# Moving the first weight chunk ahead of the activations, and a tile's transposes behind two chunks

## The chip, the cores and the metric

One core of one Trainium2 chip. The metric is the device time of one execution in microseconds; the time of a kernel is the median of several executions. Engines are TensorE (PE in the profile, its weight loads PEld), VectorE (DVE), ScalarE (ACT), GpSimd (POOL) and SyncE (SP), which issues most DMAs.

## The reference

A matrix product and a rotary embedding of each head. Shapes: x is 16 x 512 x 768, weight 768 x 768, cos and sin 512 x 64, all float32, with 12 heads of 64.

```python
y = np.matmul(x, weight).reshape(batch, seq, n_heads, head_dim)
y1, y2 = y[..., :32], y[..., 32:]
out1 = y1 * cos1 - y2 * sin1
out2 = y2 * cos2 + y1 * sin2
out = np.concatenate([out1, out2], axis=-1).reshape(batch, seq, hidden)
```

cos1, cos2, sin1, sin2 are the two halves of cos and sin, one row for each sequence position.

## The kernel before

x is worked on in 64 tiles of 128 rows by 768 columns, four tiles to a group of 16. A tile goes through these steps: it is loaded as float32 (`load`, 384 KB), cast to float16 (`castx`, on ScalarE), transposed by TensorE into PSUM in six blocks of 128 x 128 and copied from there to SBUF (`turn`, whose second argument names the engine of the copy), and multiplied by the weight. The weight is cut into six chunks of 128 rows (w0 to w5, 384 KB each, `load_w`), each cast to float16 by `cast_w`. The product of a tile is the sum over the six chunks. The tile's products lie in PSUM banks of 512 columns; `rope` multiplies them by cos and sin on VectorE and adds the two halves on GpSimd, and `store` issues the result's DMA.

Every engine works through its own instructions in the order in which the program gives them. The helper `Flow.do` gives each instruction the semaphore waits that follow from what it reads and writes, so an instruction that waits holds up what stands behind it on its engine. All loads of the first stage stand in SyncE's queue in the order of the list `order` (L441), then cos and sin, then further tiles of x, as `pump` sends them.

The first group (tiles 0 to 3) is written out by hand (L509 to L534), because the weight arrives chunk by chunk at the same time. `mm0(i, c)` multiplies tile i by chunk c in two matmuls, one of 512 columns and one of 256. `warm(k)` issues k matmuls on a tile of zeros. The order there, engine by engine:

- TensorE: nine warm matmuls, transposes of tile 0, three warm matmuls, transposes of tile 1, tiles 0 and 1 by w0, transposes of tile 2, tiles 0 and 1 by w1, then by w2, tile 2 by w0 and w1, transposes of tile 3, tile 2 by w2, then tiles 0, 1 and 2 by w3 and by w4. Behind the list come tiles 0, 1 and 2 by w5 (L591 to L593) and tile 3, with the transposes of tiles 4 and 5 between.
- VectorE: the copies of tiles 0 and 1, then the casts of w0 to w5, then two instructions that build the table from cos and sin (L535 to L539), then the products of `rope`.
- ScalarE: the casts of tiles 0, 1 and 2, the copy of tile 2, the cast of tile 3, the copy of tile 3, then casts and copies of later tiles in turn.

From tile 4 on (the loop after L602) TensorE multiplies with half-height matmuls (`both`, `steps`, profile line L349), transposes come from `turn_rows` (L257) and, for some pairs of tiles, from VectorE. Profile lines of the helpers: L176 is every cast and copy (`copy`), L196 the load of a tile of x, L218 that of a weight chunk, L242 the transposes of `turn`, L324 the matmuls of `mm0`, L394 the products and L410 the additions of `rope`.

## Time and profile before

| what | value |
|---|---|
| median of 3 executions | 154.4 us (154.16 to 154.4) |
| the profiled execution, in all | 154.73 us |
| its span, first to last instruction | 152.9 us |
| granted TensorE clock, mean | 0.994 |
| bytes moved | 51.27 MB, mean 335 GB/s |
| first x tile cast (ScalarE) begins | 4.24 us |
| w0 cast (VectorE) begins | 7.67 us |
| w5 cast begins | 14.49 us |
| first product of rope (VectorE) begins | 15.83 us |

The span and all positions are of the one profiled execution; the median is of other executions of the same kernel. In the views, L and a number is a line of the kernel, a name such as "xt<-pt" says what is written from what, and the time in brackets is how long the engine was idle before the instruction and what ended that. A wait for several things is put down to the one that came last.

### The profile page before, as it was taken

Reading aid. Unit: us, or ns where it says so; the run is one execution under the profiler, and the core shown is the slowest. Engines: PE = TensorE matmul, PEld = TensorE weight load, DVE = VectorE, ACT = ScalarE, POOL = GpSimd, SP = SyncE. Lnnn points to the kernel's source line nnn. Section 1 sums busy time; section 2 is a strip of 40 time slices with the busy share of each in tenths; the row PEclk is TensorE's granted clock in tenths of the full one; section 3 lists DMA queues with packets and bytes.
Section 4 is the critical chain, followed back from the end, with each engine's and each line's share of the span. In section 5 each row is a group of like instructions: output and inputs, shape, how many; then the busy total and the mean of one; then the engine's idle time right before and its main releaser. Section 6 shows DMA issues by size and latency. Waiting matters only on the chain.

```text
span 152.9 us, 4416 instructions
## 1 busy us (share of the span) xinstructions
PE 141.5 (93%) x1944; PEld 102.7 (67%) x1944; DVE 129.3 (85%) x119; ACT 78.7 (51%) x92; POOL 124.6 (81%) x81
## 2 busy tenths in 40 slices
PE   6669997999999999999999999999999999999930
PEld 2325674777777778777777777777777777766720
DVE  0244995888888999999999999999999999978980
ACT  3444778879778843556263726273526735461000
POOL 1000299599999999999999999999997979799970
PEclk9999999999999999999999999999999999999997
DMA  3999999999999999999999999999999998550992
GB/s 124 350 395 404 400 402 385 385 380 257 363 358 352 368 336 353 349 400 340 339 341 392 364 336 339 372 370 334 345 360 407 416 403 323 233 210 0 374 354 97
DMA packets 27555, 51.27 MB, mean 335 GB/s; under 512 B 7184, under 2 KB 13072, under 8 KB 27536
## 3 DMA queue, kind: packets, MB, share of 16 engines
q1 hardware_dynamic: 13504, 24.78, 46.8%
q10 hardware_dynamic: 8592, 24.25, 40.3%
q0 software_dynamic: 5440, 1.97, 10.4%
q8 instruction: 15, 0.25, 0.6%
q14 instruction: 4, 0.03, 0.1%
HBM read 27.79 MB, written 25.17 MB: 346 GB/s over the span
## 4 chain that ended last, share of the span: by engine, by line
PE 86%; DMA 5%; DVE 3%; SPq 1%; ACT 1%; issue 1%; DVEq 0%
PE py L349 72%; PE py L324 8%; DMA w_raw<-in_weight_dram 5%; PE pt L257 4%; PE pt L242 1%; DVE w_raw L394 1%; SPq L196 1%; DVE ov L410 1%; SPq L218 1%; ACT xc L176 1%; ACT xt L176 1%; DVE xs L394 0%; DVE w_sb L176 0%; DVE tq L394 0%; DVEq L57 0%
## 5 line engine op out<-in xcount | busy, mean ns | idle before, releaser
L349 PE MATMUL py<-w_sb,xt 64*128 64x512 f16 (+1 forms) x864 | 95.6, 323 | 0.0
L410 POOL TENSOR_TENSOR ov<-tq 128x1024 f32<-128x1024 f32 (+2 forms) x33 | 68.9, 2109 | 19.3 <-DVE tq L394 19.1
L394 DVE TENSOR_TENSOR tq<-py,csn 128x1024 f32<-128x1024 f32 (+2 forms) x56 | 68.1, 1253 | 3.6 <-PE py L349 3.1
L349 PEld LDWEIGHTS py<-w_sb,xt 64*128 64x128 f16 x864 | 58.8, 94 | 17.2
L349 PE MATMUL py<-w_sb,xp 64*128 64x512 f16 (+1 forms) x480 | 61.9, 323 | 0.0
L176 ACT COPY xt<-pt 128x768 f16<-128x768 f16 x42 | 33.5, 799 | 39.4 <-PE pt L257 27.3
L176 ACT CAST xc<-xs 128x768 f16<-128x768 f32 x44 | 39.1, 902 | 21.1 <-DMA xs<-in_x_dram 17.2
L394 DVE TENSOR_TENSOR w_raw<-py,csn 128x1024 f32<-128x1024 f32 (+1 forms) x38 | 45.3, 1191 | 5.3 <-PE py L349 3.7
L410 POOL TENSOR_TENSOR ov<-w_raw 128x1024 f32<-128x1024 f32 (+2 forms) x22 | 44.3, 2027 | 3.4 <-DVE w_raw L394 3.2
L349 PEld LDWEIGHTS py<-w_sb,xp 64*128 64x128 f16 x480 | 35.5, 94 | 9.9
L324 PE MATMUL py<-w_sb,xt 128*128 128x256 f16 (+1 forms) x96 | 15.5, 313 | 1.9 <-DVE w_sb L176 1.7
L257 PEld LDWEIGHTS pt<-ident,xc 64*128 64x128 f16 x432 | 13.7, 95 | 2.7 <-ACT xc L176 1.4
L324 PEld LDWEIGHTS py<-w_sb,xt 128*128 128x128 f16 x96 | 8.7, 98 | 7.5 <-DVE w_sb L176 3.2
L257 PE MATMUL pt<-ident,xc 64*128 64x64 f16 x432 | 12.6, 190 | 1.1 <-ACT xc L176 1.1
L211 POOL DMA_DIRECT2D xh<-in_x_dram x20 | 11.7, 594 | 0.0
L176 ACT CAST xd<-xb 128x1536 f16<-128x1536 f32 x5 | 8.2, 1630 | 1.5 <-DMA xb<-in_x_dram 1.4
L176 DVE CAST w_sb<-w_raw 128x768 f16<-128x768 f32 x6 | 3.4, 560 | 4.4 <-DMA w_raw<-in_weight_dram 4.4
L285 DVE STREAM_TRANSPOSE xp<-xh 128x768 f32<-128x768 f32 x5 | 6.2, 1235 | 0.0
L492 PE MATMUL py<-cold 128*128 128x512 f16 x12 | 4.3, 518 | 1.4 <-DVE cold L435 1.4
L176 DVE COPY xt<-pt 128x768 f16<-128x768 f16 x2 | 1.1, 557 | 4.9 <-PE pt L242 4.9
L285 DVE STREAM_TRANSPOSE xp<-xd 128x768 f32<-128x768 f32 x5 | 4.8, 969 | 0.0
L242 PEld LDWEIGHTS pt<-ident,xc 128*128 128x128 f16 x48 | 3.0, 98 | 2.7 <-ACT xc L176 1.8
(16 smaller groups left out, 13.2 us busy)
## 6 DMA issues: line engine op xcount, KB each, us to landing
out_dram<-ov ACTq DMA_DIRECT2D x30, 768.0 KB, 8.8
xs<-in_x_dram SPq DMA_DIRECT2D x44, 384.0 KB, 15.9
xb<-in_x_dram SPq DMA_DIRECT2D x20, 192.0 KB, 18.0
w_raw<-in_weight_dram SPq DMA_DIRECT2D x6, 384.0 KB, 7.8
xh<-in_x_dram POOLq DMA_DIRECT2D x20, 96.0 KB, 13.7
out_dram<-ov SPq DMA_DIRECT2D x1, 384.0 KB, 3.1
out_dram<-ov ACTq DMA_DIRECT2D x1, 384.0 KB, 2.8
out_dram<-ov SPq DMA_DIRECT2D x1, 256.0 KB, 2.1
```

The costliest lines, as they stand in the source:

```text
L176: eng.copy(out=o, in_=i_) if e == "act" else eng.tensor_copy(out=o, in_=i_)
L196: do(e, lambda eng: eng.dma_start(out=xs_b[k], in_=x[b].rearrange("(p r) h -> r p h", r=SB)[r]), writes=[f"xs{k}"], dma=f"xs{k}")
L211: do(e, lambda eng: eng.dma_start(out=dst[ts(q, R)], in_=src[r, q]), writes=[f"{name}q{q}"], dma=name)
L218: do(e, lambda eng: eng.dma_start(out=w_raw[:, t, h], in_=wv[t, h]), writes=[f"wr{t}{h}"], dma=f"w{t}{h}")
L242: do("pe", lambda eng: eng.transpose(pt[:, t, h, :], src[:, t, h, :], ident), reads=[f"xc{c}", "ident"], writes=[f"pt{k}"], tick=(t, h) == ...
L257: do("pe", lambda eng: eng.transpose(pts[r][:, t, h, :], src[rows, t, h, :], ident[rows, rows]), reads=[f"xc{c}", "ident"], writes=[f"pt{r ...
L285: do("dve", lambda eng: eng.transpose(out=dst, in_=src), reads=rd, writes=[f"xp{z}"])
L324: do("pe", lambda eng: eng.matmul(ps, get(t, h), w_sb[:, t, h, a - s * H : z - s * H], start=start, stop=stop), reads=[key, f"w{t}{h}"], w ...
L349: do("pe", lambda eng: eng.matmul(py[:, lo:hi], get(t, h)[rows], w_sb[rows, t, h, lo - s * H : hi - s * H], start=opens, stop=r == 1 and s ...
L394: do("dve", lambda eng: eng.tensor_tensor(out=tq.rearrange("p j (h d) -> p j h d", d=D), in0=ps.rearrange("p (h d) -> p h d", d=D) .unsque ...
L410: do(adder, lambda eng: eng.tensor_tensor(out=ov_b[o][:, ds(c0, w)].rearrange("p (h t d) -> p h t d", t=2, d=HD), in0=tq[:, 0].rearrange(" ...
L492: do("pe", lambda eng: eng.matmul(py[:, ts(b, 512)], cold[:, 0:P], cold, start=True, stop=warmed[0] < WARM - 6), reads=["cold"], writes=[f ...
```

## The change

w0 is issued ahead of all tiles of x. Its cast moves on VectorE to the front, ahead of the copies of tiles 0 and 1. On TensorE tiles 0 and 1 are multiplied by w0 and w1 before the transposes of tile 2. The copy of tile 2 moves from ScalarE to VectorE, where it stands between the casts of w1 and w2. Tile 2 is multiplied by w0 and w1 before tiles 0 and 1 are multiplied by w2. What follows the transposes of tile 3 stays.

```diff
-    order = [0, 1, "w0", 2, "w1", "w2", 3, "w3", "w4", "w5"]
+    order = ["w0", 0, 1, "w1", 2, "w2", 3, "w3", "w4", "w5"]
...
     U0 = units(0)
     warm(9)
+    cast_w(CHUNKS[0], "dve")
     castx(0, "act")
     turn(0, "dve")
     castx(1, "act")
     warm(3)
     turn(1, "dve")
     castx(2, "act")
-    cast_w(CHUNKS[0], "dve")
     for i in (0, 1):
         mm0(i, CHUNKS[0])
-    turn(2, "act")
+    cast_w(CHUNKS[1], "dve")
+    for i in (0, 1):
+        mm0(i, CHUNKS[1])
+    turn(2, "dve")
     castx(3, "act")
-    for c in CHUNKS[1:3]:
-        cast_w(c, "dve")
-        for i in (0, 1):
-            mm0(i, c)
+    cast_w(CHUNKS[2], "dve")
     for c in CHUNKS[:2]:
         mm0(2, c)
+    for i in (0, 1):
+        mm0(i, CHUNKS[2])
     turn(3, "act")
     mm0(2, CHUNKS[2])
     for c in CHUNKS[3:5]:
```

## The prediction

> **What bounds the kernel now.** I read the page first: span, busy shares, chain by line.

> ```profile
> span 152.9 us, 4416 instructions
> PE 141.5 (93%) x1944; PEld 102.7 (67%) x1944; DVE 129.3 (85%) x119; ACT 78.7 (51%) x92; POOL 124.6 (81%) x81
> ...
> PE 86%; DMA 5%; DVE 3%; SPq 1%; ACT 1%; issue 1%; DVEq 0%
> ```

> TensorE is busy 93% of the span and holds 86% of the chain that ends last; all the DMA on that chain is the load of one weight chunk. So the steady part is TensorE's, and the edit, which lies before 16 us, is worth what it does to the moment at which TensorE's unbroken run reaches a given instruction. The chain in order of time shows where that run begins and the only place where it breaks again before the tail:

> ```profile
> 3.28 7.27 DMA w_raw<-in_weight_dram
> ...
> 10.57 0.57 DVE w_sb L176
> ...
> 11.19 1.47 PE py L324 x8
> 12.66 0.33 PE pt L242 x6
> 12.99 4.24 PE py L324 x26
> ...
> 23.42 0.80 ACT xt L176
> 24.22 0.80 ACT xc L176
> ```

> Columns are start, length, what. The DMA step ends at 10.54: this is chunk w2. From 11.19 TensorE goes on without a wait: eight matmuls, the transposes of tile 3, 26 matmuls. A unit for later: one tile times one chunk is two matmuls, so 26 matmuls are 13 units in 4.24 us, 0.326 us each; one tile's transposes take 0.33.

> Next the timeline of the first 18 us, VectorE, ScalarE and weight loads, for landings and slack (start, length, instruction; in brackets the idle time before it and what ended it):

> ```profile
> 4.24 1.84 ACT L176 CAST xc<-xs 128x768 f16<-128x768 f32 x2 [2.05 <-DMA xs<-in_x_dram]
> 6.77 0.56 DVE L176 COPY xt<-pt 128x768 f16<-128x768 f16 x1 [0.43 <-PE pt L242]
> 7.67 0.56 DVE L176 CAST w_sb<-w_raw 128x768 f16<-128x768 f32 x1 [0.34 <-DMA w_raw<-in_weight_dram]
> 8.62 0.87 ACT L176 CAST xc<-xs 128x768 f16<-128x768 f32 x1 [2.55 <-DMA xs<-in_x_dram]
> 9.58 0.56 DVE L176 CAST w_sb<-w_raw 128x768 f16<-128x768 f32 x1 [1.35 <-DMA w_raw<-in_weight_dram]
> 10.10 0.80 ACT L176 COPY xt<-pt 128x768 f16<-128x768 f16 x1 [0.60 <-PE pt L242]
> 14.49 0.56 DVE L176 CAST w_sb<-w_raw 128x768 f16<-128x768 f32 x1 [0.45 <-DMA w_raw<-in_weight_dram]
> 15.11 1.74 PEld L324 LDWEIGHTS py<-w_sb,xt 128*128 128x128 f16 x12 [0.23 <-DVE w_sb L176]
> 17.16 0.34 PEld L242 LDWEIGHTS pt<-ident,xc 128*128 128x128 f16 x6 [0.31 <-ACT xc L176]
> ```

> A cast starts some 0.02 us after its transfer lands, so by place in the queue the landings are about 4.22 (place 1), 5.17 (place 2: issued at 1.39, 3.8 us to landing), 7.65 (3, now w0), 8.60 (4, x2), 9.56 (5, w1), 10.54 (6, w2), then about 0.97 apart to 14.47 (10, w5). One interval is out of line: place 3 comes 2.48 us after place 2 instead of 0.95, so 1.53 us late, and all later places keep that lag. Two more things are to be seen. The load of w5's first weights begins at 15.11, just when w5's cast (14.49 + 0.56, and 0.06 that TensorE takes to start) is done: TensorE, from 11.19, needs 0.65 + 0.65 + 0.33 + 0.33 + 0.98 + 0.98 = 3.92 us to come to w5, that is 15.11. There is **no slack**, and a faster head alone gains nothing while w5 lands at 14.47. And tile 4's transposes at 17.16 wait for ScalarE's cast of x4 (16.22 to 17.11): six units after 15.11 would be 17.07, so a head that is late gets 0.09 us back there.

> In whole-microsecond windows the traffic of the lag is seen (busy of each engine, then granted clock, DMA share, GB/s):

> ```profile
> 4.00:5.00 1.00, 0.93 (x4) 0.19 (x2) 0.00 (x0) 0.76 (x1) 0.00 (x0) 1.00 0.99 387
> 5.00:6.00 1.00, 0.74 (x8) 0.56 (x9) 0.21 (x1) 0.93 (x2) 0.00 (x0) 1.00 1.03 338
> 6.00:7.00 1.00, 0.73 (x8) 0.42 (x6) 0.57 (x2) 0.08 (x1) 0.00 (x0) 1.00 0.96 289
> 9.00:10.00 1.00, 0.56 (x7) 0.34 (x6) 0.42 (x1) 0.49 (x1) 0.00 (x0) 1.00 1.02 406
> ```

> **The change, part by part.** *The queue order.* All ten transfers are 384 KB and go through SyncE's queue; w0 goes from place 3 to 1, x0 to 2, x1 to 3, w1 from 5 to 4, x2 from 4 to 5; w2 to w5, x3 and all behind keep place and bytes. I take the landings by place, because the dip to 338 and 289 GB/s lies at a time (5 to 7 us) when transfers of both kinds are under way, and because x and w transfers keep the same 0.95 to 0.98 us spacing afterwards. Bounds for x1, which takes place 3: 6.12 if the lag belonged to w0 standing there (5.17 + 0.95), 8.60 if it slipped a further place. I use 7.65, the row of that place.

> *The early cast of w0* (0.56 us) runs at 4.24 to 4.80, while VectorE would idle until the first transposes are done: nothing. Behind it in VectorE's order stands the copy of tile 0, not due before 6.65; w0 would have to land after 6.0 to cost anything.

> *The path through x1.* x0: cast 5.19 to 6.07, transposes 6.12, copy done 7.21, beside the wait for x1. x1: cast 7.67 to 8.54 (0.87), transposes from 8.60, copy 0.54 after their start (as 9.55 to 10.10 now), 9.14 to 9.70. w1's cast, landed at 8.60, stands behind that copy in VectorE's order: 9.72 to 10.28. TensorE does tile 1 by w0 at 9.76, both tiles by w1 from 10.34 to 10.99, and only then, in its own order, tile 2's transposes; x2's cast (9.58 to 10.45) has been ready for half a microsecond. VectorE's copy of tile 2 starts at 11.53 and ends at 12.09 (ScalarE needs 0.80 for it now, so VectorE saves 0.24, which is in the sum). TensorE goes on at 12.15 with tile 2 by w0 and w1.

> *The path through w2.* Its cast, ready at 10.54, now stands in VectorE's order behind the copy of tile 2, which waits for transposes: 12.11 to 12.67 instead of 10.57 to 11.13. Waiting for it is TensorE alone, at 12.80, after tile 2 by w0 and w1; so this wait costs nothing, with 0.07 us of cover. Without cover it would cost its 0.56.

> From 12.15 the same 3.92 us of work stand between TensorE and w5 as now from 11.19: the same units in another order. So w5 begins at 16.07 instead of 15.11: **+0.96**, and at tile 4's transposes 0.09 of it is regained: **+0.87**. The moved copy takes 0.80 us from ScalarE, which idles there (0.65 to 2.55 us before each of its casts there): nothing. VectorE's first product, now at 15.83 and tied to cos and sin, would come at 16.7, so 0.9 late with TensorE; TensorE's next use of those banks, now at 18.94, comes after VectorE's release at 18.12, and both shift together. The break at 23.4 doesn't swallow it: the two ScalarE steps there (copy, cast) begin when TensorE's own transposes end. After 25.07 the chain is TensorE to the tail.

> [...] The copy of a transposed tile out of PSUM took 0.56 us on VectorE and 0.80 on ScalarE in the rows above. [...]

> The sum against the profiled execution: 152.9 span, 154.73 in all, would become 153.8 and 155.6. The median of the runs shown is 154.4, 0.33 below that execution; on it the forecast is 154.4 + 0.87 = **155.3 us**.

> **Rivals.** (a) *x1 in time, x2 late.* If x1 lands by 6.8, the path through x2 decides: place 5 is 0.96 later than place 4. x2 9.56, cast to 10.45, transposes 10.50, copy to 11.60, TensorE 11.66 instead of 11.19: +0.47 - 0.09 = +0.38, 154.8. For it: the lag's lost bytes (62 and 111 of some 400 GB/s over 1 us each) are only 0.43 us of all the queues together, so it may sit elsewhere next time. Against it: place 3 had the lag.

> (b) *The lag goes away: faster.* If the lag belongs to the first weight rows being read behind two tiles of x, then w0 at place 1 takes it into the start-up, and places 3 to 10 land up to 1.53 us sooner: x1 at 6.12, and the whole computed path with it. Then +0.87 - 1.53 = -0.66, 153.7; it decides from x1 before 6.78 and x2 before 9.18. For it: the transfer with the lag is the first one of the weight. Against it: the dip goes on at 6 to 7 us, when x2 and w1 are due, and a queue with the same bytes is no shorter.
> [...]

> (c) *Later still.* w0's first read costs at the start and the lag comes too: x1 between 7.95 and 8.60, the sum between +1.2 and +1.8, 155.6 to 156.2. For it: only that place 1 has not been a weight before.

> (d) *Nothing*, if a later stage gives it all back: 154.4. Only the 23.4 us break could, and it follows TensorE.

> **How the numbers follow.** Forecast (+0.6 to +1.15, 155.0 to 155.55) 48%; (a) 18%; (b) 23%; (c) 8%; (d) 3%. The time is the forecast's. What can be told from no change is 0.2%, 0.31 us. Slower: 48 + 12 of (a) + 8 = 68%. Same: 6 of (a), 3 of (b), 3 of (d) = 12%. Faster: 20 of (b). The range runs from (b)'s full price, 153.7, to 155.6, where (c) begins; about 10% is left out, most of it (c).

> **What would show it.** Right: x1's cast near 7.67 and not 6.1; copies of tiles 1 and 2 near 9.1 and 11.5; w2's cast beginning right behind the latter though w2 lands at 10.5; w5's first weights near 16.0 with no wait on their cast; tile 4's transposes near 18.0 without a wait; the same gap near 24; tail unchanged, span 153.8. Wrong: x1's cast before 6.8, which brings (a) or (b), told apart by w5's landing (14.5 or near 13); a wait of TensorE for w2 would make it 0.1 or more worse.

## The result, and the profile after

| | before | changed |
|---|---|---|
| median of 20 executions | 154.39 us (153.21 to 156.32) | 155.0 us (154.37 to 155.81) |
| ratio, 95% interval | | 1.0052 (1.0031 to 1.0072) |
| the profiled execution, in all | 154.73 us | 154.79 us |
| its span | 152.9 us | 153.0 us |

The ratio is 0.80 us (0.48 to 1.11) on 154.4: slower, by half a per cent. It is taken over fast executions alone (none over 1.5% above a kernel's fastest); the medians, of all 20, are 0.61 us apart. But the profiled execution of the changed kernel is only 0.06 us longer than that of before, and the 20 times fall into two groups of ten, 154.37 to 154.79 and 155.22 to 155.81. The profile is of the lower group. Both facts have to be explained.

The page of the changed kernel, span and chain by engine:

```profile
span 153.0 us, 4416 instructions
...
PE 83%; DVE 4%; DMA 3%; POOL 3%; ACT 2%; issue 1%; SPq 1%; ACTq 0%; DVEq 0%
```

VectorE, GpSimd and ScalarE have entered the chain at TensorE's cost. Where, the chain in order of time shows (start, length, what):

```profile
1.86 4.96 DMA xs<-in_x_dram
6.85 0.89 ACT xc L176
...
10.71 0.57 DVE xt L176
...
11.32 1.48 PE py L324 x8
...
15.95 2.30 DVE tq L394
...
18.33 4.70 POOL ov L410 x2
...
23.05 0.42 ACTq L431
...
23.51 0.80 ACT xt L176
24.30 0.80 ACT xc L176
...
25.15 0.35 PE pt L257 x12
```

Instead of w2's load, the load of x1 starts the chain. TensorE's run with tile 2 begins at 11.32 behind VectorE's copy of that tile (10.71), where w2's cast at 10.57 released it before. The timeline has the landings (start, length, instruction, idle time before and what ended it):

```profile
6.85 0.88 ACT L176 CAST xc<-xs 128x768 f16<-128x768 f32 x1 [0.82 <-DMA xs<-in_x_dram]
9.23 0.88 ACT L176 CAST xc<-xs 128x768 f16<-128x768 f32 x1 [1.50 <-DMA xs<-in_x_dram]
8.80 0.55 DVE L176 CAST w_sb<-w_raw 128x768 f16<-128x768 f32 x1
11.18 0.55 DVE L176 CAST w_sb<-w_raw 128x768 f16<-128x768 f32 x1
14.13 0.56 DVE L176 CAST w_sb<-w_raw 128x768 f16<-128x768 f32 x1 [0.43 <-DMA w_raw<-in_weight_dram]
```

x1 landed at 6.83, not at 7.65; x2 at 9.21; w5's cast began at 14.13 instead of 14.49. So this execution's loads had a smaller lag than those of the profile before, by 0.36 us. That hides the cost. TensorE's rows of the loop over tiles 4 and up (its first matmul of L349) and of the transposes behind the break, in the profile before:

```profile
18.94 1.89 PE L349 MATMUL py<-w_sb,xt 64*128 64x512 f16 x10
25.07 0.35 PE L257 MATMUL pt<-ident,xc 64*128 64x64 f16 x12 [1.07 <-ACT xc L176]
```

and in the changed one:

```profile
18.94 1.90 PE L349 MATMUL py<-w_sb,xt 64*128 64x512 f16 x10
25.15 0.35 PE L257 MATMUL pt<-ident,xc 64*128 64x64 f16 x12 [1.15 <-ACT xc L176]
```

The loop begins at 18.94 in both. Counted from the start of w5's cast, which carries the whole lag, it begins after 4.45 us before and after 4.81 now, and the transposes behind the break come after 10.58 and 11.02. **Freed of the lag, the change costs 0.36 us at the loop and 0.44 behind the break.** This distance is the measure used below.

### The profile page after: what moved, and what is told of

Its sections match the earlier page's. It is cut to its first block, busy times and chain, and to the rows that moved or that the text cites. A ratio compares the mean times of both kernels' runs of the same rounds, so it can differ in the third digit from the quotient of the medians.

```text
span 153.0 us, 4416 instructions
## 1 busy us (share of the span) xinstructions
PE 141.8 (93%) x1944; PEld 102.9 (67%) x1944; DVE 129.5 (85%) x120; ACT 78.1 (51%) x91; POOL 124.6 (81%) x81
## 4 chain that ended last, share of the span: by engine, by line
PE 83%; DVE 4%; DMA 3%; POOL 3%; ACT 2%; issue 1%; SPq 1%; ACTq 0%; DVEq 0%
PE py L349 70%; PE py L324 7%; PE pt L257 4%; DMA xs<-in_x_dram 3%; POOL ov L410 3%; DVE tq L394 2%; PE pt L242 1%; ACT xc L176 1%; DVE w_raw L394 1%; DVE xt L176 1%; DVE ov L410 1%; ACT xt L176 1%; DVE xs L394 0%; SPq L196 0%; ACTq L431 0%
## 5 line engine op out<-in xcount | busy, mean ns | idle before, releaser
L349 PE MATMUL py<-w_sb,xt 64*128 64x512 f16 (+1 forms) x864 | 95.6, 323 | 0.0
L349 PEld LDWEIGHTS py<-w_sb,xt 64*128 64x128 f16 x864 | 58.8, 94 | 17.3
L349 PE MATMUL py<-w_sb,xp 64*128 64x512 f16 (+1 forms) x480 | 61.9, 323 | 0.0
L176 ACT COPY xt<-pt 128x768 f16<-128x768 f16 x41 | 32.8, 800 | 44.1 <-PE pt L257 31.2
L176 ACT CAST xc<-xs 128x768 f16<-128x768 f32 x44 | 39.2, 903 | 18.6 <-DMA xs<-in_x_dram 14.4
L349 PEld LDWEIGHTS py<-w_sb,xp 64*128 64x128 f16 x480 | 35.5, 94 | 9.9
L324 PE MATMUL py<-w_sb,xt 128*128 128x256 f16 (+1 forms) x96 | 15.6, 313 | 1.0 <-DVE xt L176 1.0
L324 PEld LDWEIGHTS py<-w_sb,xt 128*128 128x128 f16 x96 | 8.9, 98 | 6.4 <-DVE xt L176 1.5
L176 ACT CAST xd<-xb 128x1536 f16<-128x1536 f32 x5 | 8.2, 1634 | 0.0
L176 DVE CAST w_sb<-w_raw 128x768 f16<-128x768 f32 x6 | 3.3, 556 | 4.1 <-DMA w_raw<-in_weight_dram 4.1
L242 PEld LDWEIGHTS pt<-ident,xc 128*128 128x128 f16 x48 | 3.0, 98 | 3.5 <-issue 1.6
L176 DVE COPY xt<-pt 128x768 f16<-128x768 f16 x3 | 1.7, 557 | 4.4 <-PE pt L242 4.4
L242 PE MATMUL pt<-ident,xc 128*128 128x128 f16 x48 | 4.0, 220 | 1.4 <-ACT xc L176 1.4
```

The source lines that it names most:

```text
L176: eng.copy(out=o, in_=i_) if e == "act" else eng.tensor_copy(out=o, in_=i_)
L242: do("pe", lambda eng: eng.transpose(pt[:, t, h, :], src[:, t, h, :], ident), reads=[f"xc{c}", "ident"], writes=[f"pt{k}"], tick=(t, h) == ...
L324: do("pe", lambda eng: eng.matmul(ps, get(t, h), w_sb[:, t, h, a - s * H : z - s * H], start=start, stop=stop), reads=[key, f"w{t}{h}"], w ...
L349: do("pe", lambda eng: eng.matmul(py[:, lo:hi], get(t, h)[rows], w_sb[rows, t, h, lo - s * H : hi - s * H], start=opens, stop=r == 1 and s ...
```

## The experiments

Of each profiled execution (us; "distance" is from the start of w5's cast to the loop's first matmul):

| kernel | x1 landed | w5's cast | loop | distance | in all |
|---|---|---|---|---|---|
| before | 5.17 | 14.49 | 18.94 | 4.45 | 154.73 |
| before, again | 5.26 | 14.43 | 18.84 | 4.41 | 155.19 |
| changed | 6.83 | 14.13 | 18.94 | 4.81 | 154.79 |
| changed, again | 6.71 | 13.91 | 18.72 | 4.81 | 154.75 |
| changed, third | 6.42 | 13.79 | 19.62 | 5.83 | 155.42 |
| loads' order alone | 6.46 | 13.67 | 18.39 | 4.72 | 154.88 |
| order of work alone | 5.67 | 13.85 | 18.98 | 5.13 | 155.61 |
| copy on ScalarE | 6.58 | 13.75 | 18.93 | 5.18 | 155.18 |
| x1 later | 8.04 | 14.51 | 20.86 | 6.35 | 156.91 |
| more warm matmuls | 7.03 | 13.88 | 19.04 | 5.16 | 154.88 |

### Each part alone

The order of the loads alone: the kernel before with

```diff
-    order = [0, 1, "w0", 2, "w1", "w2", 3, "w3", "w4", "w5"]
+    order = ["w0", 0, 1, "w1", 2, "w2", 3, "w3", "w4", "w5"]
```

> Only the order of the loads is changed (w0 ahead of all tiles of x, x2 at place 5); the order of work on the engines is that of before. My theory (the time is set by when TensorE has tile 2, and a queue place is worth 0.96 us): TensorE, which transposes tile 2 ahead of tiles 0 and 1 by w1, waits for x2's cast; with landings as in the profile of before, transposes at 10.50, w1's matmuls 10.83 to 11.48, w2's at 11.48 instead of 11.19, so +0.29 and 0.09 regained at tile 4: +0.2 us against before. Rival (the moved loads are the whole cost, the reordered work costs nothing): +0.6 us, as the full change.

Distance 4.72, so +0.27 against 4.45, near the +0.2 of the theory, but by another wait (TensorE's rows):

```profile
9.14 0.82 PE L324 MATMUL py<-w_sb,xt 128*128 128x512 f16 x4 [1.12 <-DVE w_sb L176]
9.80 0.50 PE L242 MATMUL pt<-ident,xc 128*128 128x128 f16 x6
```

Tile 2's transposes didn't wait for x2's cast, which was done at 9.68. TensorE had waited for w0's cast: w0 landed at 4.57, but in the old order of work its cast stands on VectorE behind the copies of tiles 0 and 1, and began at 8.54. Both paths came to tile 2 within 0.1 us of each other, so the agreement is luck. The time, 154.52 against 154.88 (ratio 0.9981, 0.9927 to 1.0036), can't tell +0.2 from nothing, but speaks against +0.6.

The order of work alone: the changed kernel with the old line `order`.

> Only the order of work on the engines is changed; the loads stand as before. My theory: tile 2's transposes wait behind tiles 0 and 1 by w1, whose cast ends at 10.14, so they begin at 10.85 instead of 9.55, the copy ends at 11.95 and the unbroken run of TensorE, from tile 2 by w0 on, begins at 12.0 instead of 11.19: +0.8 less 0.09, +0.7 us against before. Rival (the loads are the whole cost): 0.0. A second rival, that the copy on VectorE is what costs: then w2's cast, behind it in VectorE's order, would be waited for by TensorE; I expect no such wait.

Distance 5.13, +0.68, as expected; the time doesn't contradict (1.0032, 0.9964 to 1.0101). There was no wait for w2's cast. So each half costs by itself, 0.27 and 0.68 (one execution of each), and the two together only 0.36. In the new order of work tile 2's transposes wait for tiles 0 and 1 by w1, and the new loads bring w1 a place sooner; with the new loads w0 is early, and the new order of work casts it early. Each half needs the other.

### The same kernels again

> The kernel before, unaltered, for a second profile. My theory: from the start of w5's cast to the first matmul of the loop 4.45 us again, 0.36 below the changed kernel, whatever the lag of the loads is in this execution; the lag itself (w5's cast at 14.49 in the first profile, 13.67 to 14.14 in the others) moves by some tenths from execution to execution. Rival: the figure moves with the lag.

4.41 with a lag nearly like the first's: it agrees, though it hardly tests the rival. What tests it is the whole table: with the first group of before (also in the three kernels further down that leave it as it is) the distance is 4.40 to 4.45 while w5's cast moves from 13.86 to 14.49. TensorE stood still in this execution behind a late load near 117 us (in the chain the load ends at 116.09 and TensorE goes on at 117.78), which is why it took 155.19.

> The changed kernel, unaltered, for a second profile: where do x1, w1 and x2 land in another execution? My theory of the two groups of its times (near 154.7 and near 155.5): they differ in x1's landing; an execution near 154.7 has x1 before 6.9 and tile 2 set by x2, one near 155.5 has x1 near 7.65 and TensorE coming to tile 2 by w0 near 12.1. Rival: the groups differ in the tail or the steady part, and the first 18 us are alike.

Again the lower group (154.75): distance 4.81, x1 at 6.71. No execution of the upper group was caught yet.

### The copy's engine, and x1's place

```diff
-    turn(2, "dve")
+    turn(2, "act")
```

> The changed kernel with the copy of tile 2 back on ScalarE. My theory (tile 2's path from x2's landing, then TensorE's unbroken run): the copy takes 0.80 instead of 0.56, so TensorE's run begins 0.24 later against the loads; from the start of w5's cast to the first matmul of the loop 4.81 + 0.24 = 5.05 us. Rival (w2's cast, which stands behind the copy on VectorE, is what TensorE waits for): with the copy gone from VectorE the cast comes sooner and the figure falls below 4.8.

5.18: later by 0.37, where 0.24 was expected from the copy. Here TensorE came to tile 2's transposes at 9.93, and x2's cast had ended at 9.74. x0 had landed only at 5.64, and its transposes (6.67) and the three warm matmuls behind them held up those of tile 1 to 7.65. So the path through the first tiles set the time, and this is the other 0.13. The sign settles it: w2's cast was free sooner and nothing got faster, so that wait costs nothing, and VectorE is the cheaper place for this copy (0.56 us there, 0.80 on ScalarE).

x1 a place further back:

```diff
-    order = ["w0", 0, 1, "w1", 2, "w2", 3, "w3", "w4", "w5"]
+    order = ["w0", 0, "w1", 1, 2, "w2", 3, "w3", "w4", "w5"]
```

> The changed kernel with x1 one place further back: w0, x0, w1, x1, x2, the rest as it is. It makes the case that the prediction forecast, tile 1 late. My theory: TensorE's unbroken run begins 4.50 us after x1 lands; x1 lands 5.84 us ahead of w5, so from the start of w5's cast to the first matmul of the loop it is 4.81 + 1.45 = 6.3 us, less at most 0.1. Rival: only the order of work on the engines counts, 4.8.

6.35, but not for the reason given. Here w5's cast was itself held up in VectorE's order, to 14.51 though w5 landed at 13.86; from the landing the loop is 7.0 us away. By x1's landing TensorE should have come to tile 2 by w0 at 12.4 to 12.5 and came at 13.25. The missing 0.8 us is in the windows of this run (busy of each engine, then granted clock, DMA share, GB/s):

```profile
8.00:9.00 1.00, 0.01 (x1) 0.01 (x1) 0.00 (x0) 0.87 (x1) 0.00 (x0) 0.71 0.98 387
9.00:10.00 1.00, 1.00 (x7) 0.75 (x8) 0.15 (x1) 0.88 (x1) 0.00 (x0) 0.50 1.05 421
10.00:11.00 1.00, 0.99 (x4) 0.21 (x3) 0.87 (x2) 0.08 (x1) 0.00 (x0) 0.50 1.01 406
11.00:12.00 1.00, 1.00 (x5) 0.58 (x5) 0.00 (x0) 0.80 (x1) 0.00 (x0) 0.59 1.05 421
12.00:13.00 1.00, 0.60 (x8) 0.32 (x5) 0.36 (x1) 0.00 (x0) 0.00 (x0) 1.00 1.01 384
```

The clock granted to TensorE fell to 0.50 between about 8.4 and 11.8 us (0.71 over one microsecond is 0.58 us at half clock, 0.59 is 0.82 us), while tile 1 was late and TensorE had stood idle for 1.5 us (busy for 0.51 between 7 and 8 us, 0.01 between 8 and 9). A theory that the prediction didn't have: **the gaps that the change opens in TensorE's first microseconds act on its clock.**

### The upper group

> The changed kernel, unaltered, for a third profile. From the start of w5's cast to the first matmul of the loop 4.81 us again; x1 lands before 7.1 again and tile 2's copy is released by the path through x2. If this execution is of the group near 155.5, it has a wait of 0.5 to 0.8 us behind a load near 117 us that the two profiles near 154.8 don't have; the rival is a later head.

This execution, 155.42 (one more beside the 20), is of the upper group, and the rival is right: no wait behind a load near 117 us, but a distance of 5.83. x1 was early (6.42), so the theory that the groups differ in its landing falls. TensorE's rows of this run:

```profile
6.34 0.80 PE L242 MATMUL pt<-ident,xc 128*128 128x128 f16 x6 [0.92 <-ACT xc L176]
6.93 1.49 PE L492 MATMUL py<-cold 128*128 128x512 f16 x3
8.21 0.85 PE L242 MATMUL pt<-ident,xc 128*128 128x128 f16 x6
...
10.86 0.50 PE L242 MATMUL pt<-ident,xc 128*128 128x128 f16 x6
```

and the first three of the same in the first profile of the changed kernel:

```profile
6.17 0.49 PE L242 MATMUL pt<-ident,xc 128*128 128x128 f16 x6 [0.88 <-ACT xc L176]
6.50 0.81 PE L492 MATMUL py<-cold 128*128 128x512 f16 x3
7.78 0.51 PE L242 MATMUL pt<-ident,xc 128*128 128x128 f16 x6 [0.47 <-ACT xc L176]
```

The same instructions take 0.80, 1.49 and 0.85 instead of 0.49, 0.81 and 0.51. From start to start the three warm matmuls are 0.43 us apart here and 0.22 there: TensorE still runs at half the rate it has there. In this execution tile 1's transposes wait not for x1's cast, done at 7.32, but for TensorE's slow work ahead of them; tile 2 by w0 begins at 12.01 instead of 11.1 to 11.3, and the loop 0.68 to 0.90 us later than in the other two.

The column of the granted clock in the views shows 1.00 from the start in all these runs (in the third also from 7 to 8 us, where the warm matmuls are 0.43 us apart) but hides the half rate: the trace's record of the clock begins with its first rise. That rise stands at 4.29 and 4.16 us in the two profiles of before, and at 5.02, 5.92 and 10.08 in the three of the changed kernel. Between the nine warm matmuls and tile 0's transposes TensorE was idle for 0.75 to 0.92 us in these three, because x0 lands a place later (its cast begins at 5.16 to 5.33 instead of 4.24 and 4.36); in the two of before, that gap was 0.33 and 0.52 us.

The changes of the clock in these records have a spacing. With x1 later the clock is up from 5.00 to 8.41, at half from there to 11.82 and up again: 3.41 us each. In the 13 other profiles the time from its rise to its fall behind the last matmuls is 41 to 44 times 3.413 us (146.77 us, in the first profile of either kernel, is 43 times). What sets this spacing, no run shows. But each profile can be laid out in stretches of 3.413 us, back from the rise, and the share of each that matmuls fill can be read from the trace:

| execution | stretch (us) | filled by matmuls | the clock at its end |
|---|---|---|---|
| before | 0.87 to 4.29 | 0.84 | rises |
| changed | 1.60 to 5.02 | 1.00 | rises |
| changed, again | 2.50 to 5.92 | 0.86 | rises |
| changed, third | 3.25 to 6.66 | 0.73 | stays down |
| changed, third | 6.66 to 10.08 | 1.00 | rises |
| x1 later | 5.00 to 8.41 | 0.42 | falls |

In all 14 profiles the stretch that ends at a rise is filled to 0.81 or more, and none filled to 0.73 or less ends at one. Once up, the clock stayed up behind stretches of 0.46 and more. In the third execution a stretch took in the whole gap, and the clock rose one stretch later. My reading of these profiles: **where the stretches fall against the gap makes the two groups.**

The 20 executions bear this out. In the profiles the clock falls to half behind the last matmuls at the end of such a stretch and stays there, so the span and the mean clock of an execution give an estimate of the time of the fall: 153.0 - 2 x 0.004 x 153.0 = 151.8 us for the profiled one, where the trace has 151.79. Carried back by whole stretches (good to about 0.15 us), each execution has one stretch that ends between 4.08 and 7.49 us. In eight it ends behind 6.05 us, with most or all of the gap inside, and all eight are of the upper group (155.44 to 155.81). Of the other twelve, ten are of the lower group. The two that are not took 155.73, with an end at 4.15 (TensorE starts at 1.41, so that stretch is filled to 0.80, between the 0.73 and the 0.81 of the profiles), and 155.22, with 5.71, which stays open. The kernel before shows no such split: of its 55 executions that are compared in the experiments, 28 have the end behind 6.05 and a median of 154.40, the other 27 one of 154.56.

A half clock alone isn't enough: with the old first group it was seen twice (tile 0's transposes 0.80 us, in the kernel with tiles 7 and 8 cast sooner and in the one with the pairs on SyncE, further down) and cost nothing, distances 4.44 and 4.42, because the clock had risen by tile 1's transposes (0.50) and the work behind waits for loads there (TensorE was idle for 1.12 us ahead of tiles 0 and 1 by w0 in the former). To test it, the gap was filled:

```diff
-    WARM = 12
+    WARM = 14
...
-    warm(9)
+    warm(11)
```

> The changed kernel with eleven warm matmuls ahead of tile 0's transposes instead of nine. In the third profile of the changed kernel the transposes of tile 0 took 0.80 us and the three warm matmuls 1.49, against 0.49 and 0.81 in the other two: TensorE still ran at half clock there, after it had stood idle from 5.4 to 6.3 us, and came 0.7 us later to the loop. My theory: the group near 155.5 is made of such executions, and the idle time that w0's place in front opens is what keeps the clock down in them; two more matmuls of 0.43 us at half clock fill it to about 6.1 us, so the clock is up by 7 us in every execution, the distance from w5's cast to the loop is 4.8 to 4.9 and times between 155.2 and 155.9 come only with late loads: the median is 0.3 to 0.5 us below the changed kernel's 155.0 against the same kernel before, that is a ratio to before of 1.002 to 1.004 instead of 1.0052. Rival: the clock's rise has nothing to do with the idle time; the ratio stays at 1.005 or, as the added matmuls hold up tile 0, grows.

Ratio to before 1.0011 (0.9981 to 1.0040), below the 1.002 to 1.004 expected, median 154.68 against 154.45. Of the 11 executions that are compared, ten lie between 154.42 and 155.14 and one at 155.68, so the upper group is nearly gone; its profile has the rise at 5.88 and the full clock at tile 0's transposes (0.49). Three of the 11 have their stretch end at 6.48, 6.78 and 7.00, where the changed kernel had upper executions alone, and they took 154.65, 155.00 and 154.62; the one at 155.68 isn't among them (5.28). (One further execution took 307.86 us; it wasn't profiled and its cause is open.) Its distance of 5.16 is more than the 4.8 to 4.9 expected: x1 landed late here, at 7.03. The intervals of the two ratios overlap, so the size of the gain over the changed kernel is open; that the gap made the upper group is borne out.

### Where the first loads lose time

```diff
+    do("act", lambda eng: eng.dma_start(out=seen_sb[:, 0:128], in_=wv[0, 0][:, 0:128]), ...
+    do("act", lambda eng: eng.dma_start(
+        out=seen_sb[:, 128:256], in_=x[2].rearrange("(p r) h -> r p h", r=SB)[0][:, 0:128]), ...
```

> The kernel before, and ahead of its loads two small loads of 64 KB each on ScalarE's queue, the first 512 bytes of 128 rows of the weight and of x2, into a buffer that nothing reads. Theory 1 (the lag of 1.2 to 1.5 us belongs to a time, or to the queue, whatever is read): the third landing stays near 7.65 or is up to 0.3 later for the added 128 KB; 0 to +0.3 us. Theory 2 (the lag is the first read of a region of memory): the third landing comes near 6.4 and w5's near 13.4, and the time falls by 0.7 to 1.1 us.

The first tile now landed at 5.07 instead of 4.22, the third transfer at 7.24, the rest 0.96 to 1.02 apart, and w5's cast began at 14.14. A lag is still there but in another place; it is no smaller than in runs without the small loads. Theory 2 isn't borne out, and theory 1's "third landing" isn't either. 155.89 against 154.88 (1.0075, 1.0013 to 1.0138) is slower; the one profile has three waits behind loads between 100 and 119 us (0.19, 0.24 and 1.02 us) and nothing at the head, where the distance is 4.40. What makes the lag is open.

### Does the loss have to reach the end?

The break near 24 us was closed in the kernel before:

```diff
+                if n == 3 * i + 1 and i == QB + 1:
+                    turns(8, 1)
...
+        if i == QB:
+            casts(8, 1)
         turns(i + 1 + (T_AHEAD if i > QB + 1 else 2), 1)
+        if i == QB:
+            casts(9, 1)
...
-        if s == 0 and g > 0:
+        if s == (1 if g == 1 else 0) and g > 0:
```

> The kernel before, its loads and first group untouched; at tile 4 ScalarE casts tiles 7 and 8 around the copy of tile 6 instead of after it, tile 7's transposes go one step earlier on TensorE, and the first store of group 0 goes behind them. It tries the other theory of what the profiles show: between 23.7 and 25.1 TensorE stands still for 1.4 us in every run, and the chain there goes through ScalarE's copy, cast and store. If that break is free-standing, it is closed and the end comes 0.8 to 1.4 us sooner: -0.8 us or better. Rival: the loads set the pace behind it, and the gain is given back before 140 us: 0.0.

The break was gone, and nothing was won: 154.74 against 154.55 (1.0005, 0.9970 to 1.0040). The rival is right; the profile shows where it went (ScalarE, then TensorE):

```profile
98.50 0.91 ACT L176 CAST xc<-xs 128x768 f16<-128x768 f32 x1 [4.21 <-DMA xs<-in_x_dram]
...
100.16 0.35 PE L257 MATMUL pt<-ident,xc 64*128 64x64 f16 x12 [0.92 <-ACT xt L176]
```

The cast of a tile waited 4.2 us for its load, and TensorE behind it. With the same edit in the changed kernel:

> The changed kernel, with tiles 7 and 8 cast sooner. With the break at 24 us closed TensorE meets late loads near 99 and 108 us. My theory: loads set a floor there, so the 0.48 us by which the change makes TensorE later at the head is swallowed, the waits near 99 and 108 us are that much shorter, and the time is within 0.3 us of that of the same edit without the change. Rival: the head's cost is carried to the end, +0.5 us.

0.9996 (0.9958 to 1.0035), against 1.0005 without the change: no 0.5 us between them, but the intervals are wide enough to hold it, and in the two profiles the loop still ended 0.47 us apart (137.78 and 138.25). But its twelve executions don't split by the clock's stretches either: the six with an end behind 6.05 have a median of 154.53, the other six one of 154.93, where the changed kernel's groups are 0.85 apart. That speaks for a loss that is swallowed; it isn't settled.

What holds the loads back near 100 us was tried once. In the profile before, the DMA engines between 90 and 118 us (packets, MB, share):

```profile
q10 hardware_dynamic: 1822, 5.30, 47.9%
q1 hardware_dynamic: 2559, 4.06, 43.5%
q0 software_dynamic: 1802, 0.65, 18.7%
```

With tiles 7 and 8 cast sooner, the pairs of q0 were given to SyncE:

```diff
-        BLOCKS[g, 1] = "pool" if g % 2 == 0 and g >= 4 else "sp"
+        BLOCKS[g, 1] = "sp"
```

> The kernel with tiles 7 and 8 cast sooner (first group and first loads as before), and the five tile pairs that GpSimd loads with a cast are loaded by SyncE as the other pairs are and cast on ScalarE. Between 90 and 118 us the DMA engines are busy throughout, and GpSimd's queue takes 18.7% of their time for 0.65 MB of 10.06. My theory of the late waits (near 99, 108 and 117 us TensorE stands still for 0.4 to 1.3 us behind loads of x): with that share gone the loads land sooner, the waits go, and the gain of the closed break at 24 us stays: -1.0 us or better against before. Rival: the wait is not the loads' rate but what ScalarE has to do (five casts of 1.6 us more); then the waits stay or grow, 0.0 or slower.

Slower, 158.95 against 155.12 (1.0241, 1.0178 to 1.0305). My theory fell: TensorE was busy for 17.15 us of those from 80 to 100, against 19.24 with the pairs on GpSimd, and the chain by engine says what it waited for:

```profile
DMA 33%; PE 32%; SPq 24%; ACT 3%; DVE 3%; issue 3%; DVEq 0%
```

Loads are 33% of the chain now, and SyncE's issuing, 1% before, is 24%. ScalarE, which the rival named, has 3%: the time is as the rival said, but its cause isn't seen. No kernel tried here is measurably faster than the kernel before.

## Why the prediction was right, and where it was not

**Slower, by this order.** Forecast +0.87 us and 155.3; measured +0.80 by the ratio (0.48 to 1.11) and +0.61 by the medians, median 155.0. The direction holds. That the size fits is luck: the measured figure is a mixture of +0.30 and +1.15 in about equal parts, and neither was made of the terms of the sum.

**Held.** No slack before w5: the distance is 4.40 to 4.45 in every run with the old first group. The two paths to tile 2: x1's landing + 4.50 and x2's + 2.10 were forecast; 6.71 to 11.11 is 4.40, 7.03 to 11.43 (more warm matmuls) is 4.40, and 9.21 to 11.32 (the profile above) is 2.11. The 0.10 by which the first was too long lies in w1's cast, which starts 0.47 us after the copy ahead of it (8.33 and 8.80) where the sum has 0.58. w2's cast behind the copy, w0's early cast and the work taken off ScalarE cost nothing. The loss passes through the break at 24 us.

**The step that failed: "I use 7.65, the row of that place".** x1 landed at 6.83, 6.71 and 6.42 in three executions of the changed kernel. The lag of the first loads exists in all runs but doesn't belong to place 3; part of it came at place 4 (in the first of them w1 landed near 8.2, 1.4 us behind x1, where places are 0.95 to 0.98 apart elsewhere). That makes rival (a) the case at the head: +0.38 forecast, +0.36 measured as distance. x1's path and x2's are nearly level there: in the first profile tile 2's transposes waited 0.09 us for x2's cast, in the second they followed TensorE's own work. Taking one execution's landing for a property of the queue was the error; the second profile of before has x1's place at 7.31.

**A term left out, 0.09 us.** The path through the break is no longer TensorE's alone: VectorE's first product starts 1.82 us after w5's cast instead of 1.34, GpSimd's additions follow, and the store that waits for them on ScalarE's queue (23.05) holds the copy behind it. So the loss is 0.44 to 0.48 there instead of 0.36.

**A mechanism left out: the clock.** x0's place was costed at nothing "beside the wait for x1". But it opens up to 0.92 us of idle TensorE while the clock is down, and in the third profile, where one stretch takes all of that in, the clock rises at 10.08 us instead of 5.02 and 5.92. The groups' medians are 154.69 and 155.54, that is 0.30 and 1.15 above that of before; the forecast's 0.87 lies between them, where one execution of 20 fell (155.22).

## What to carry to other kernels

Move a transfer in a queue, and every transfer that it passes comes one place later, here by 0.95 to 0.98 us where no lag falls: ask of each what idles meanwhile, and whether that engine's clock has risen yet. The gap of 0.75 to 0.92 us that was opened here ahead of tile 0's transposes went with a distance of 4.81 in two executions and of 5.83 in a third, so judge such a gap by many executions. A lag read from one execution is a price for that execution (7.65 was forecast for x1's landing, 6.42 to 6.83 measured); compare kernels from an event behind the lag (here the last weight chunk), not from the start. And lay warm-up work out for the latest landing of what the first real instruction needs, not for the usual one: here two more matmuls, which cut the gap to 0.18 us, left one execution of 11 above 155.2 us, where the changed kernel had ten of 20.
